# A recorded kernel's scheduling model with table loads and landing times, and one more query tile of stick-breaking attention turned by VectorE squares and a transfer

## The chip, the core and the metric

The kernel runs on one core of a Trainium2 chip. A core has a matrix engine (TensorE, PE in the profile), VectorE (DVE), ScalarE (ACT), GpSimd (POOL) and SyncE (SP), which here only issues transfers. Each engine works through its own queue of instructions in order; an instruction that waits holds up all behind it. The metric is device time in microseconds, the median over several runs; lower is better.

## What is computed

One layer of a hybrid encoder: 1024 prompt rows and 32 sample rows of width 1024. Cut to what matters here:

```python
def stick_breaking(q, k, v, q_pos, k_pos):
    z = jnp.einsum('bqhd,bkhd->bhqk', q, k).astype(jnp.float32) * ATTN_SCALE
    causal = (k_pos[None, :] < q_pos[:, None])[None, None]
    log_beta = jax.nn.log_sigmoid(z)
    log_1m = jnp.where(causal, jax.nn.log_sigmoid(-z), 0.0)
    after = lax.cumsum(log_1m, axis=3, reverse=True) - log_1m
    w = jnp.where(causal, jnp.exp(log_beta + after), 0.0).astype(v.dtype)
    return jnp.einsum('bhqk,bkhd->bqhd', w, v)

def reference(...):
        qa, ka, va, ga, qb, kb, vb, gb = in_proj(hp, g_pre[i], w_in[i])
        oa = mixer_a_prompt(qa, ka, va, rel_bias[i])
        ob = mixer_b_prompt(qb, kb, vb)
        hp = finish(hp, oa, ga, ob, gb, w_out[i], g_post[i], p_prompt[i], w_ple[i], w_ple_gate[i])
        ...
```

`in_proj` is an RMS norm and one projection to 4096 columns. Eight heads of width 64 (A) use banded softmax attention with a position bias, eight (B) the stick-breaking attention above. `finish` gates both results, projects them, normalizes, and adds a gated embedding. The sample rows go through the same, with caches of keys and values.

## The kernel before

**Stages.** After a start that normalizes and turns the input, the kernel goes through four pairs of heads of A and four of B in turn (A0, B0, A1, B1, ...; `B21` is the second head of pair 2 of B). Beside a pair's attention run the projection columns of the next pair (`mm_kA`, `mm_qB`, ... 24 matmuls of 352 columns for each third of the rows), and beside the last pair the gates (`mm_gA`, `mm_gB`). A last stage, closed off from the first, holds both square projections (`o0P` to `g3P`), in seven products of half-size blocks. All matrix work runs on numbers split into a high and a low part, so most things exist twice (`kd`/`kl`, `wTh`/`wTl`).

**A head of B.** Its 1024 queries are eight tiles of 128 rows; tile i sees i + 1 blocks of 128 keys. `scores(i)` (L828) makes two matmuls per piece into PSUM (`SB`), VectorE adds the mask of the diagonal block, ScalarE takes the sigmoid into `om`, VectorE runs a product scan backwards over it, and GpSimd subtracts neighbours into `be`: the weights, queries on the partitions. `weights_t(i)` (L878) turns them so that keys are on the partitions and splits them into `wTh` and `wTl`. `values(g)` (L928) multiplies the turned tiles 0 to 3 (g = 0) or 4 to 7 (g = 1) with V into `PVB`; it needs all four tiles of its group. A head of A is alike, with a bias, an exponential, and at most 5 blocks for a tile.

**Two ways to turn a tile.** The usual way: TensorE turns each 128x128 block against the identity into PSUM (`ptwB`, `ptwA`), up to four blocks to a bank; ScalarE casts the bank into `wTh`, VectorE subtracts that from the bank into `wTl`. The other way is for tiles named in `ROUND` (L31): VectorE turns 32x32 squares of the whole tile from `be` to `om`, SyncE writes `om` to a scratch tensor in HBM (`swapB<-om`), then reads it back by four transfers, one for each quarter of the partitions (`be<-swapB`); ScalarE casts `be` into `wTh`, and VectorE subtracts SBUF from SBUF into `wTl`. Before the change tiles 4 and 6 of each head, of A and of B, go this way. `om` and `be` are ring buffers (L517) of 3076 and 3328 columns for all heads; a tile's part is handed on when its last use is over. The PSUM pools have two banks for the projection (`mm`), three for scores, two for turned blocks, one for values (L473).

**What sets the order.** Nothing is issued as the code runs. `Recorder` (L264) notes each operation with its operands; `Recorder.add` (L308) finds what it depends on and calls `cost` (L338) for its duration and the delay until its result is usable. `Recorder.order` (L374) then simulates the five engines with these numbers: at each step the engine that is free first takes the ready operation with the smallest key (attention before projection columns on TensorE, then order of recording). The sequence that comes out is emitted as the program. So the constants in `cost` and `order` decide only in which order each engine's instructions stand. For a transfer, the model before takes `ISSUE` = 600 ns of SyncE's time, and lets data be there after a further 1500 ns, the time of the bytes, and a margin of 2000 ns. Loads of ScalarE's function tables are no operations of the recorder: they come into the program where `Exp` follows `Sigmoid` or the other way round, and the model before has no time for them. `shared` marks operations on the port that VectorE and GpSimd share.

Of the kernel before, what the change touches and what calls it, by code (L numbers as in the profile page):

```python
# [8 lines left out]
F32 = mybir.dt.float32  # L9
F32R = mybir.dt.float32r  # L10
AF = mybir.ActivationFunctionType
# [16 lines left out]

ROUND = {"A": ((4,),(6,)), "B": ((4,),(6,))}  # L31
LAG_T = 2
LAG_V = 2
SPACE_S = 0.1
# [138 lines left out]


class Op:
    __slots__ = ("eng", "what", "args", "kw", "key", "busy", "late", "ready", "left", "after", "at", "size", "shared")


LAND = {"PE": 165, "ACT": 0, "DVE": 0, "POOL": 0, "SP": 0, "CTL": 0}
SEM = 60  # L180
MARGIN = 400
ISSUE = 600
DMA_NS, DMA_RATE, DMA_MARGIN = 1500, 320.0, 2000
DVE_SET, POOL_SET = 137, 110


# [77 lines left out]
class Recorder:  # L264
# [35 lines left out]
    def node(self, eng, what, args, kw, after):  # L300
        o = Op()
        o.eng, o.what, o.args, o.kw, o.after = eng, what, args, kw, after
        o.key = (self.cls if eng == "PE" else self.low, len(self.ops))
        o.shared = False
        self.ops.append(o)
        return o

    def add(self, eng, what, args, kw):  # L308
        writes, reads = [], []
        method = what[1] if isinstance(what, tuple) else ""  # L310
        for i, a in enumerate(args):
            if isinstance(a, (View, Raw, Segments)):
                (writes if i == 0 or (method == "tensor_tensor_reduce" and i == 7) else reads).append(a)
        for k, a in kw.items():
            if isinstance(a, (View, Raw, Segments)):
                (writes if k in ("out", "accum_out") else reads).append(a)
        o = self.node(eng, what, args, kw, set())
        for mine, write in ((reads, False), (writes, True)):
            for v in mine:
                b = v.buf  # L320
                hit = False
                for other, box, wrote in b.uses:
                    if other is not o and (write or wrote) and all(p < y and x < q for (p, q), (x, y) in zip(v.box, box)):
                        o.after.add(other)
                        hit = True
                if b.pool is not None:
                    if not hit:
                        o.after.add(b.place)
                    b.pool.ops.append(o)
                b.uses.append((o, v.box, write))  # L330
        o.busy, o.late = self.cost(eng, method, args, kw, writes, reads)
        o.shared = eng == "POOL"
        if eng == "DVE":
            sbuf = [v for v in reads if isinstance(v, (View, Segments)) and not v.buf.psum and v.free() > 4]
            o.shared = len(sbuf) > 1 or (method == "tensor_copy" and len(sbuf) == 1 and not writes[0].buf.psum)

    @staticmethod
    def cost(eng, method, args, kw, writes, reads):  # L338

        out = writes[0] if writes else None  # L340
        n = out.free() if isinstance(out, View) else 1
        psum = any(isinstance(v, (View, Segments)) and v.buf.psum for v in reads)
        if eng == "PE":
            if method == "transpose":
                return (109 if args[1].shape[0] > 64 else 62), 165
            return max(109.0, 2.5 + 0.449 * args[2].free()) * (1 if args[2].buf.dtype == F32R else 4), 165
        if eng == "ACT":
            return (60 if psum else 95) + 0.83 * n + (190 if "accum_out" in kw else 0), 105
        if eng == "DVE":
            if method == "tensor_tensor_scan":  # L350
                return 120 + 2.1 * n, 85
            if method == "tensor_copy" and not psum:
                return 70 + 0.53 * n, 85
            if method == "scalar_tensor_tensor":
                return 125 + 1.04 * n, 85
            if method == "tensor_tensor_reduce":
                return 90 + 1.04 * n, 150
            return 70 + 1.04 * n, 85
        if eng == "POOL":
            if method == "tensor_tensor":  # L360
                if n == 1:
                    return 535, 40
                return 170 + (1.77 if out.buf.dtype == F32 else 2.15) * n, 40
            if method == "tensor_scalar":
                return 255 + 0.86 * n, 0
            return 100 + 0.82 * n, 0
        size, run = 4, 0
        for v in (out, args[1]):
            if isinstance(v, View) and v.buf.pool is not None:
                size, run = 4 * v.shape[0] * v.free(), 4 * v.shape[-1]  # L370
        return ISSUE, max(size / DMA_RATE, size / run * (8.5 + 0.0365 * run) / 16)


    def order(self):  # L374

        import heapq
        for place, old in self.turns:
            place.after.update(x[0] for x in old.uses)
        users = {id(o): [] for o in self.ops}
        for o in self.ops:  # L380
            o.left, o.ready = len(o.after), 0.0
            for a in o.after:
                users[id(a)].append(o)
        names = ("PE", "ACT", "DVE", "POOL", "SP", "CTL")
        free = dict.fromkeys(names, 0.0)
        soon = {e: [] for e in names}
        now = {e: [] for e in names}
        for o in self.ops:
            if not o.left:
                heapq.heappush(soon[o.eng], (0.0, o.key, id(o), o))  # L390
        out, port, line = [], 0.0, 0.0
        while len(out) < len(self.ops):
            best = None
            for e in names:
                if now[e]:
                    t = free[e]
                elif soon[e]:
                    t = max(free[e], soon[e][0][0])
                else:
                    continue  # L400
                if best is None or t < best[0]:
                    best = (t, e)
            t, e = best
            while soon[e] and soon[e][0][0] <= t:
                _, key, n, o = heapq.heappop(soon[e])
                heapq.heappush(now[e], (key, n, o))
            o = heapq.heappop(now[e])[2]
            if o.shared and e == "DVE" and port > t + DVE_SET:
                held = [x for x in now[e] if not x[2].shared]
                if held:  # L410
                    heapq.heappush(now[e], (o.key, id(o), o))
                    pick = min(held)
                    now[e].remove(pick)
                    heapq.heapify(now[e])
                    o = pick[2]
            o.at = t
            if e == "CTL":
                done = t
            elif e == "SP":
                free[e] = t + o.busy  # L420
                line = max(line, t + o.busy + DMA_NS) + o.late
                done = line + DMA_MARGIN
            else:
                if o.shared:
                    t = max(t, port - (DVE_SET if e == "DVE" else POOL_SET))
                    port = t + o.busy
                free[e] = t + o.busy
                done = t + o.busy + o.late
            out.append(o)
            for u in users[id(o)]:  # L430
                if u.eng == e and e != "SP":
                    r = t if e == "CTL" else free[e] if e == "PE" else done
                else:
                    r = done + (0 if u.eng == "CTL" else SEM + (MARGIN if u.eng == "PE" else 0))
                u.ready = max(u.ready, r)
                u.left -= 1
                if not u.left:
                    heapq.heappush(soon[u.eng], (u.ready, u.key, id(u), u))
        return out
# [18 lines left out]
def stream_step(  # L458
# [79 lines left out]
    def load_w(j):  # L538

        if j >= len(order) or j in raws:  # L540
            return
        kind, p = order[j]
        c0 = NAMES.index(kind) * 512 + p * P
        raws[j] = []
        for kh in range(2):
            raw = wpool.tile([P, 4, P], F32, tag="wr", name=f"wr_{kind}{p}_{kh}", bufs=4)
            dma(raw, w_in[0, kh * 512:(kh + 1) * 512, c0:c0 + P].rearrange("(k p) c -> p k c", p=P))
            raws[j].append(raw)
# [243 lines left out]
    def attention(ab, p, h):  # L792
# [16 lines left out]

        together = {i: g for g in ROUND[ab] for i in g}  # L810
        whole, done_with = {}, []
# [901 lines left out]
    for m, (nm, src, group) in enumerate(sets):  # L1713
        last_set = m == len(sets) - 1
        state = [{}, {}]
        for n, prod in enumerate(ORDER):
            for pair, t in enumerate(group):
# [43 lines left out]
                if nm == "o":  # L1761
# [4 lines left out]
                    if prod == "P6":  # L1766
                        add(up, st["p1"], bank, ALU.add)
# [101 lines left out]
```

## Time and profile before

| | us |
|---|---|
| median of 3 runs | 805.05 (804.86 to 805.52) |
| the profiled execution | 809.23 |
| its span, first to last instruction | 807.4 |
| ScalarE's table loads, 10 of 1283 ns | 12.8 |

The profile is of one execution. The span is 1.8 us shorter than that execution's own time, and the profiled execution is 4.2 us longer than the median of the others. The rows below are of these kinds: the page's busy time by engine and by slice (40 equal slices, each digit a busy share in tenths); busy time by stretch; waits (who waited for whom: us in total, times, longest); groups of instructions (engine, operation, `out<-in`, size, count | busy us, mean ns of one | idle time before them and what ended it); and the timeline (start us, duration us, engine, operation, count, and in brackets the idle time before it). `SPq` is SyncE's queue; a transfer's row there is its issue, and the rows of issues end with the median us from issue to landing. Matmuls are pipelined, so their durations overlap.

### The profile page before, as it was taken

The page shows a single profiled execution, that of the slowest core. Times are in us where ns is not written, and L with a number is a line of the kernel's source. Part 1 is how long each engine was busy: PE and PEld are TensorE (multiplying, and loading weights), DVE is VectorE, ACT ScalarE, POOL GpSimd, SP SyncE. Part 2 cuts the span into 40 slices and gives each one's busy share as a digit, 9 for nine tenths or more (in the row PEclk, how much of TensorE's full clock was granted, in tenths as well). Part 3 has the DMA queues.
Part 4 walks back from the last instruction along what each step waited for, and adds up shares of the span by engine and source line. Part 5 has one row for each costly group of instructions (what it writes and reads, how often), then busy time and mean ns, then how long its engine had stood idle before and what let it go on. Part 6 is the DMA issues. An engine that isn't in the chain of part 4 may idle for free.

```text
span 807.4 us, 14271 instructions
## 1 busy us (share of the span) xinstructions
PE 788.0 (98%) x4646; PEld 722.3 (89%) x4646; DVE 567.9 (70%) x1007; ACT 504.4 (62%) x1061; POOL 432.1 (54%) x503
## 2 busy tenths in 40 slices
PE   8999989999999999999999999999999999999997
PEld 7899989899989999899999989999997777878786
DVE  7626768786588788788886688765435787477655
ACT  5636774676586646795675696543327977877641
POOL 5623655764356668134551236777542549598513
PEclk9999999999999999999999999999999999999999
DMA  8419895667878749854535667765569948869633
GB/s 276 149 45 293 215 253 175 195 185 217 225 225 246 215 121 267 216 146 133 151 81 169 147 175 212 234 199 152 166 207 322 298 147 270 278 218 302 215 108 131
DMA packets 160973, 161.09 MB, mean 199 GB/s; under 512 B 39154, under 2 KB 120794, under 8 KB 160899
## 3 DMA queue, kind: packets, MB, share of 16 engines
q1 hardware_dynamic: 160898, 160.18, 67.1%
q8 instruction: 37, 0.61, 0.3%
q14 instruction: 38, 0.30, 0.1%
HBM read 99.23 MB, written 52.49 MB: 188 GB/s over the span
## 4 chain that ended last, share of the span: by engine, by line
PE 72%; DMA 6%; ACT 6%; POOL 5%; DVE 5%; issue 4%; SPq 2%; DVEq 0%; POOLq 0%; ACTq 0%
PE mm_gA L452 6%; PE mm_gB L452 6%; PE mm_kA L452 5%; PE mm_qA L452 5%; PE mm_qB L452 4%; PE SB L452 3%; PE mm_vA L452 3%; PE PVB L452 3%; PE mm_kB L452 3%; PE PVA L452 3%; PE mm_vB L452 3%; PE SA L452 2%; PE o1P L452 2%; PE g2P L452 2%; PE g3P L452 2%
## 5 line engine op out<-in xcount | busy, mean ns | idle before, releaser
L452 POOL TENSOR_TENSOR be<-om 128x128 f32<-128x128 f32 (+7 forms) x64 | 75.4, 1184 | 64.8 <-DVE om L452 29.0
L452 DVE TENSOR_TENSOR_SCAN om<-om,SB 128x384 f32<-128x384 f32 (+5 forms) x96 | 94.9, 1001 | 9.1 <-ACT om L452 7.4
L452 ACT ACTIVATE om<-SB 128x384 f32<-128x384 f32 (+5 forms) x96 | 44.4, 493 | 36.0 <-DVE SB L452 26.9
L452 ACT ACTIVATE be<-om,statA 128x640 f32<-128x640 f32 (+3 forms) x64 | 44.4, 694 | 18.2 <-DVE statA L452 11.0
L452 DVE TENSOR_TENSOR wTl<-be,wTh 128x640 fp32r<-128x640 f32 (+1 forms) x32 | 37.6, 1175 | 10.3 <-ACT wTh L452 8.8
L452 ACT CAST wTh<-ptwB 128x512 fp32r<-128x512 f32 (+3 forms) x64 | 29.5, 481 | 19.6 <-PE ptwB L452 15.4
L452 DVE TENSOR_TENSOR wTl<-ptwB,wTh 128x512 fp32r<-128x512 f32 (+3 forms) x64 | 33.7, 545 | 10.3 <-ACT wTh L452 7.8
L452 DVE TENSOR_TENSOR wTl<-ptwA,wTh 128x512 fp32r<-128x512 f32 (+2 forms) x64 | 29.8, 483 | 15.7 <-ACT wTh L452 12.5
L452 POOL TENSOR_TENSOR oB<-oB,oB 128x256 f32<-128x256 f32 x32 | 27.7, 882 | 18.6 <-DMA oB<-in_w_out_dram 10.5
L452 DVE STREAM_TRANSPOSE om<-be 128x640 f32<-128x640 f32 (+1 forms) x32 | 28.9, 904 | 9.8 <-POOL be L452 4.9
L452 PE MATMUL SB<-kdB,LB 128*128 128x384 f32 (+5 forms) x96 | 34.0, 357 | 1.6 <-DVE om L452 1.6
L452 DVE CUSTOM_DVE_ANT_0 om<-SA,biasA 128x320 f32<-128x320 f32 (+3 forms) x64 | 29.5, 482 | 7.6 <-PE SA L452 4.4
L452 ACT CAST wTh<-ptwA 128x512 fp32r<-128x512 f32 (+2 forms) x64 | 26.2, 426 | 13.3 <-PE ptwA L452 7.5
L452 PE MATMUL SB<-klB,LB 128*128 128x384 f32 (+5 forms) x96 | 32.9, 345 | 0.0
L452 PE MATMUL SA<-kdA,LA 128*128 128x320 f32 (+2 forms) x96 | 30.2, 325 | 0.7 <-DVE LA L452 0.4
L452 POOL TENSOR_TENSOR sggA<-sggA,oggA 128x352 f32<-128x352 f32 x24 | 23.8, 991 | 11.2 <-DVE sggA L452 10.8
L452 PE MATMUL SA<-klA,LA 128*128 128x320 f32 (+2 forms) x96 | 29.6, 320 | 0.0
L452 ACT CAST wTh<-be 128x640 fp32r<-128x640 f32 (+1 forms) x32 | 25.0, 782 | 6.4 <-DMA swapA<-om 3.3
L452 PE MATMUL ptwB<-ident,be 128*128 128x128 f32 x192 | 28.7, 273 | 0.0
L452 PE MATMUL ptwA<-ident,be 128*128 128x128 f32 x160 | 26.3, 276 | 2.0 <-ACT be L452 1.8
L452 DVE TENSOR_TENSOR SB<-SB,maskb 128x128 f32<-128x128 f32 x64 | 17.3, 287 | 13.5 <-PE SB L452 13.1
L452 POOL TENSOR_TENSOR klA<-stkA,kdA 64x1024 fp32r<-64x1024 f32 x8 | 20.7, 2587 | 8.2 <-ACT kdA L452 7.7
(707 smaller groups left out, 2650.5 us busy)
## 6 DMA issues: line engine op xcount, KB each, us to landing
swapA<-om SPq DMA_DIRECT2D x16, 320.0 KB, 2.8
be<-swapA SPq DMA_DIRECT2D x64, 80.0 KB, 3.9
oB<-in_w_out_dram SPq DMA_DIRECT2D x16, 256.0 KB, 4.9
sum_dro<-oB SPq DMA_DIRECT2D x16, 256.0 KB, 3.3
gB<-in_w_ple_gate_dram SPq DMA_DIRECT2D x16, 256.0 KB, 4.6
sum_drg<-gB SPq DMA_DIRECT2D x16, 256.0 KB, 3.8
x<-in_x_prompt_dram SPq DMA_DIRECT2D x16, 256.0 KB, 5.2
h_dr<-h SPq DMA_DIRECT2D x8, 512.0 KB, 3.3
```

Of the source, the lines that this page charges most:

```text
L452: getattr(getattr(tc.nc, o.what[0]), o.what[1])(*args, **kw)
```

## The change

Tile 5 of each head of B is added to the tiles turned by squares and a transfer, as a group of its own. In the model, a load of a function table takes 1310 ns of ScalarE when an exponential or a sigmoid follows the other; a transfer takes 500 ns to issue and lands 2050 ns after its bytes, with no further margin; most operations of ScalarE, VectorE and GpSimd take 30 ns more, and a GpSimd operation starts 90 ns later behind one of another engine.

```diff
--- before.py
+++ after.py
@@ -28,7 +28,7 @@
 
 
 
-ROUND = {"A": ((4,),(6,)), "B": ((4,),(6,))}
+ROUND = {"A": ((4,),(6,)), "B": ((4,),(5,),(6,))}
 LAG_T = 2
 LAG_V = 2
 SPACE_S = 0.1
@@ -173,14 +173,15 @@
 
 
 class Op:
-    __slots__ = ("eng", "what", "args", "kw", "key", "busy", "late", "ready", "left", "after", "at", "size", "shared")
+    __slots__ = ("eng", "what", "args", "kw", "key", "busy", "late", "ready", "left", "after", "at", "size", "shared", "table")
 
 
 LAND = {"PE": 165, "ACT": 0, "DVE": 0, "POOL": 0, "SP": 0, "CTL": 0}
 SEM = 60
 MARGIN = 400
-ISSUE = 600
-DMA_NS, DMA_RATE, DMA_MARGIN = 1500, 320.0, 2000
+ISSUE = 500
+DMA_RATE, LANDING = 320.0, 2050
+TABLE_NS = 1310
 DVE_SET, POOL_SET = 137, 110
 
 
@@ -301,7 +302,7 @@
         o = Op()
         o.eng, o.what, o.args, o.kw, o.after = eng, what, args, kw, after
         o.key = (self.cls if eng == "PE" else self.low, len(self.ops))
-        o.shared = False
+        o.shared, o.table = False, None
         self.ops.append(o)
         return o
 
@@ -330,6 +331,7 @@
                 b.uses.append((o, v.box, write))
         o.busy, o.late = self.cost(eng, method, args, kw, writes, reads)
         o.shared = eng == "POOL"
+        o.table = next((a for a in args if a in (AF.Exp, AF.Sigmoid)), None) if eng == "ACT" else None
         if eng == "DVE":
             sbuf = [v for v in reads if isinstance(v, (View, Segments)) and not v.buf.psum and v.free() > 4]
             o.shared = len(sbuf) > 1 or (method == "tensor_copy" and len(sbuf) == 1 and not writes[0].buf.psum)
@@ -345,22 +347,22 @@
                 return (109 if args[1].shape[0] > 64 else 62), 165
             return max(109.0, 2.5 + 0.449 * args[2].free()) * (1 if args[2].buf.dtype == F32R else 4), 165
         if eng == "ACT":
-            return (60 if psum else 95) + 0.83 * n + (190 if "accum_out" in kw else 0), 105
+            return (90 if psum else 125) + 0.83 * n + (190 if "accum_out" in kw else 0), 105
         if eng == "DVE":
             if method == "tensor_tensor_scan":
-                return 120 + 2.1 * n, 85
+                return 150 + 2.1 * n, 85
             if method == "tensor_copy" and not psum:
-                return 70 + 0.53 * n, 85
+                return 100 + 0.53 * n, 85
             if method == "scalar_tensor_tensor":
-                return 125 + 1.04 * n, 85
+                return 155 + 1.04 * n, 85
             if method == "tensor_tensor_reduce":
-                return 90 + 1.04 * n, 150
-            return 70 + 1.04 * n, 85
+                return 120 + 1.04 * n, 150
+            return 100 + 1.04 * n, 85
         if eng == "POOL":
             if method == "tensor_tensor":
                 if n == 1:
-                    return 535, 40
-                return 170 + (1.77 if out.buf.dtype == F32 else 2.15) * n, 40
+                    return 565, 40
+                return 200 + (1.77 if out.buf.dtype == F32 else 2.15) * n, 40
             if method == "tensor_scalar":
                 return 255 + 0.86 * n, 0
             return 100 + 0.82 * n, 0
@@ -388,7 +390,7 @@
         for o in self.ops:
             if not o.left:
                 heapq.heappush(soon[o.eng], (0.0, o.key, id(o), o))
-        out, port, line = [], 0.0, 0.0
+        out, port, line, table = [], 0.0, 0.0, None
         while len(out) < len(self.ops):
             best = None
             for e in names:
@@ -418,20 +420,23 @@
                 done = t
             elif e == "SP":
                 free[e] = t + o.busy
-                line = max(line, t + o.busy + DMA_NS) + o.late
-                done = line + DMA_MARGIN
+                line = max(line, free[e]) + o.late
+                done = line + LANDING
             else:
                 if o.shared:
                     t = max(t, port - (DVE_SET if e == "DVE" else POOL_SET))
                     port = t + o.busy
                 free[e] = t + o.busy
-                done = t + o.busy + o.late
+                if o.table and o.table != table:
+                    table = o.table
+                    free[e] += TABLE_NS
+                done = free[e] + o.late
             out.append(o)
             for u in users[id(o)]:
                 if u.eng == e and e != "SP":
                     r = t if e == "CTL" else free[e] if e == "PE" else done
                 else:
-                    r = done + (0 if u.eng == "CTL" else SEM + (MARGIN if u.eng == "PE" else 0))
+                    r = done + (0 if u.eng == "CTL" else SEM + (MARGIN if u.eng == "PE" else 90 if u.eng == "POOL" else 0))
                 u.ready = max(u.ready, r)
                 u.left -= 1
                 if not u.left:
```

## The prediction

> **What bounds the kernel now.** I read the page's busy shares and slices first, then the busy time by stretch, then who waits on TensorE.
>
> ```profile
> span 807.4 us, 14271 instructions
> PE 788.0 (98%) x4646; PEld 722.3 (89%) x4646; DVE 567.9 (70%) x1007; ACT 504.4 (62%) x1061; POOL 432.1 (54%) x503
> ...
> PE   8999989999999999999999999999999999999997
> ...
> DVE  7626768786588788788886688765435787477655
> ...
> DMA  8419895667878749854535667765569948869633
> ```
>
> TensorE is busy in every slice. No other engine comes near, though VectorE stands mostly at 7 and 8 tenths through the attention heads (the fifth to the twenty-sixth slice), and DMA reaches 9 tenths in the fourth, sixth and sixteenth slices. A busy matmul row includes pipeline overlap, so 98% is not a statement about peak, but it says that TensorE always has something in flight: what it no longer has to issue comes off the end, unless a new wait eats it.
>
> ```profile
> 56.00:135.00 79.00, 75.78 (x478) 72.93 (x477) 53.62 (x110) 52.24 (x112) 42.22 (x53) 0.98 0.81 226
> 310.00:395.00 85.00, 84.22 (x535) 80.00 (x534) 69.89 (x133) 58.87 (x129) 39.72 (x46) 1.00 0.68 185
> ```
>
> These columns are the stretch, its length, then busy time of PE, PEld, DVE, ACT, POOL, the granted clock, DMA share and GB/s. The first stretch holds heads A00 to B00 and leaves TensorE idle for 3.2 us; the second holds the two heads of pair B2, with 0.8 us.
>
> ```profile
> PE PVA L452 <- ACT wTh L452: 2.7, 1, 2.7
> PE ptwA L452 <- ACT be L452: 1.8, 2, 1.3
> PE SB L452 <- DVE om L452: 1.6, 3, 0.9
> PE ptkA L452 <- DVE wTl L452: 1.3, 1, 1.3
> PE PVB L452 <- ACT wTh L452: 0.3, 1, 0.3
> ```
>
> So TensorE's explicit waits in the attention are few and short. Only one of them, the first, is for weights turned through a transfer; B's second value product, which needs tiles 4 to 7 of the head, has waited 0.3 us in all.
>
> **Part 1: tile 5 of B leaves TensorE.** A head's tile 5 has 6 blocks of 128x128, so 8 heads x 6 = 48 transposes go (the built program holds 4600 matmuls against 4648).
>
> ```profile
> L452 PE MATMUL ptwB<-ident,be 128*128 128x128 f32 x192 | 28.7, 273 | 0.0
> 192.18 0.93 PE L452 MATMUL ptwA<-ident,be 128*128 128x128 f32 x7
> 192.86 1.54 PE L452 MATMUL mm_kB<-hnh,wh_kB 128*128 128x352 f32 x8
> 195.04 0.60 PE L452 MATMUL ptksA<-ident,be 128*128 128x128 f32 x4
> 195.40 0.57 PE L452 MATMUL mm_kB<-hnh,wl_kB 128*128 128x352 f32 x2
> ```
>
> The mean of 273 ns is a latency; transposes overlap. Seven of them delay the next matmul by 192.86 - 192.18 = 0.68 us, four by 0.36 us: 0.09 to 0.097 each. 48 x 0.09 = 4.3 us, 48 x 0.097 = 4.7; I take 4.4. The upper end is the busy union, 28.7 / 192 = 0.149 each, 7.2 us.
>
> The Trainium skill, "TensorE: Matmul & The Clock Gate", section "Part 4: PE-mode transpose", gives about 275 ns for a transpose inside a kernel, most of it access latency. The row's 273 ns agrees as a duration; taken as a cost it would make 13 us, which is case (3) below.
>
> **Part 2: what takes its place.**
>
> ```profile
> L452 DVE STREAM_TRANSPOSE om<-be 128x640 f32<-128x640 f32 x24 | 20.1, 836 | 7.7 <-ACT be L452 4.4 <-POOL be L452 3.2
> L452 DVE STREAM_TRANSPOSE om<-be 128x896 f32<-128x896 f32 x8 | 8.9, 1107 | 2.2 <-POOL be L452 1.7 <-POOL om L452 0.4
> L452 DVE TENSOR_TENSOR wTl<-be,wTh 128x640 fp32r<-128x640 f32 x24 | 26.3, 1097 | 6.6 <-ACT wTh L452 6.3
> L452 DVE TENSOR_TENSOR wTl<-be,wTh 128x896 fp32r<-128x896 f32 x8 | 11.3, 1410 | 3.7 <-ACT wTh L452 2.4 <-DMA out_dram<-vtA 0.9
> L452 DVE TENSOR_TENSOR wTl<-ptwB,wTh 128x512 fp32r<-128x512 f32 x32 | 21.4, 680 | 8.6 <-ACT wTh L452 6.2 <-PE PVB L452 2.4
> L452 DVE TENSOR_TENSOR wTl<-ptwB,wTh 128x256 fp32r<-128x256 f32 x16 | 6.6, 413 | 0.5 <-ACT wTh L452 0.4
> L452 ACT CAST wTh<-be 128x640 fp32r<-128x640 f32 x24 | 17.4, 726 | 4.9 <-DMA swapA<-om 3.3 <-DMA be<-swapA 1.3 <-PE PVB L452 0.2
> L452 ACT CAST wTh<-be 128x896 fp32r<-128x896 f32 x8 | 7.6, 948 | 1.5 <-DMA be<-swapB 1.5
> L452 ACT CAST wTh<-ptwB 128x512 fp32r<-128x512 f32 x32 | 18.4, 587 | 16.5 <-PE ptwB L452 12.7 <-PE PVB L452 3.5
> L452 ACT CAST wTh<-ptwB 128x256 fp32r<-128x256 f32 x16 | 6.0, 376 | 1.0 <-PE ptwB L452 0.9
> ```
>
> 768 columns lie halfway between 640 and 896. VectorE gains a turn, (836 + 1107) / 2 = 972 ns, and a subtraction from SBUF, (1097 + 1410) / 2 = 1254 ns, and loses 680 + 413 = 1093 ns: +1.13 us a head, +9.0 us over the eight. ScalarE gains (726 + 948) / 2 = 837 ns and loses 587 + 376 = 963: -1.0 us in all. VectorE had 85.00 - 69.89 = 15.1 us free in the two B2 heads' stretch, which covers the 2.3 us; I put 0. Without that cover it would be up to 9.0 us. GpSimd's work on the tile is unchanged.
>
> Weighed against this is a rule of the Trainium skill, "SBUF — State Buffer", section "Who interferes with whom": a VectorE instruction with two SBUF inputs and a GpSimd instruction that reads SBUF shut each other out for a whole instruction. It speaks against the new subtraction, which reads both inputs from SBUF where the old pair read one from PSUM.
>
> ```profile
> L452 DVE TENSOR_TENSOR wTl<-be,wTh x32: 799/826/2816, 91.5 to 577.6; 128x640 fp32r<-128x640 f32 x24, 128x896 fp32r<-128x896 f32 x8
> ```
>
> By that rule, the trace agrees: minimum 799 ns, longest 2816. Should each of the eight meet the longest, VectorE would pay some 8 x (2816 - 1254) = 12.5 us more, again beside TensorE.
>
> **Part 3: the round trip, and the new landing times.** A turned tile is written out by one issue and read back by four, on SyncE's queue: 40 more issues (824 DMAs in the program against 784).
>
> ```profile
> 419.00 1.11 DVE L452 STREAM_TRANSPOSE om<-be 128x896 f32<-128x896 f32 x1
> 420.14 0.35 SPq L452 DMA_DIRECT2D swapB<-om  x1
> 422.66 1.86 SPq L452 DMA_DIRECT2D be<-swapB  x4
> 430.31 0.94 ACT L452 CAST wTh<-be 128x896 fp32r<-128x896 f32 x1
> be<-swapB SPq DMA_DIRECT2D x32, 112.0 KB, 2.9
> ```
>
> SyncE spends 0.35 + 1.86 = 2.2 us a head on it, 18 us in all. Behind those issues in its queue stand the weight loads (`wr`), the writes of `o_dr` and the swap of V; the reads wait for the write's landing, the write for the squares of the tile, and whatever stands behind waits with them. In this round the last read was issued by 424.5; with 2.9 us to land it was there at about 427.2, while the cast started at 430.3: 3 us of slack, which the old model had put there (600 + 1500 + 2000 = 4100 ns and the data for each transfer). The new one allows 500 + 2050 = 2550, so 1.55 us less for each of two transfers and 0.4 for four issues, 3.5 us: the slack is spent, and casts will stand about where the data lands. Where the data comes late, ScalarE waits at the cast with all that is behind it (score sigmoids, PSUM copies), as here:
>
> ```profile
> 103.31 0.72 ACT L452 CAST wTh<-be 128x640 fp32r<-128x640 f32 x1 [3.30 <-DMA swapA<-om]
> 104.08 1.18 PE L452 MATMUL PVA<-wTh,v2A 128*128 128x512 f32 x3 [2.73 <-ACT wTh L452]
> ```
>
> There 3.30 us on ScalarE became 2.73 us on TensorE even under the old model. In the program's order the room shrinks too: from tile 6's last score to the second value product of its head TensorE has 124 matmuls in B21 (184 before), 138 in B11 (172), 135 in B00 (156); six of each difference are the transposes. Price: at least 0 (before, B's waits are 0.3), at most 3.5 us at each of the 8 B heads, 28. The value lies near the before end, since landing stays within the allowance in a round like the one shown: +1.5, half of one busy round.
>
> **Part 4: table loads and the other constants.**
>
> ```profile
> 474.55 1.28 ACT L452 ACT_TABLE_LOAD   x1
> ...
> 477.63 0.66 PE L452 MATMUL ptwA<-ident,be 128*128 128x128 f32 x4 [1.29 <-ACT be L452]
> ```
>
> The old model knew nothing of this load, and TensorE waited 1.29 us for an exponential behind it. The new one counts 1310 ns, but it doesn't choose by it: both programs hold ten loads. The triple switch that stood at the start of B30 is gone and one stands at the start of B10, where the model now knows of it. Between -1.8 (both `ptwA` waits gone) and +1.3 (the wait moves, one more stays): I take -0.8. The added 30 ns on ScalarE, VectorE and GpSimd and 90 ns before a GpSimd instruction redraw the order everywhere; no row prices that. Its room is the rest of the listed waits, 1.6 + 1.3 + 0.3 = 3.2 us to either side; I take 0.
>
> **Sum.** -4.4 + 0 + 1.5 - 0.8 + 0 = -3.7 us. The profiled execution took 809.2 us, 1.8 more than its span, and would take 805.5; the median of the runs is 805.05, which gives 801.4. With transposes at 7.2, 0 for landing and -1.8 the low end is 805.05 - 9.0 = 796. A measurement here tells apart about 0.2%, 1.6 us.
>
> **The rivals.**
> (1) *Slower: casts in line before their data.* For it: the spent slack and the shorter room in B11, B21, B00. Against it: outside the first stretch no `wTh` cast's wait reached TensorE for more than 0.3 us. If each B head's second value product waits 1.3 us, the longest ordinary wait listed, that is 10.4 - 4.4 = +6 us, 811; at 0.8 us a head, 807. It decides from about 0.75 us a head on.
> (2) *No change: the gain is given back in the reshuffled order.* 4.4 us is little against an order redrawn for 14271 instructions; two or three new waits like the 1.3 us ones do it: 803.5 to 806.6. Against it: the five waits listed above come to 7.7 us, so a redrawn order has as many old waits to lose as new ones to find.
> (3) *More than the cadence:* if a transpose costs its whole 273 ns, 13.1 us go and 792 remains. Against it: the next matmul starts 0.36 us after four of them.
> That the change does nothing is excluded for part 1 (the instructions are gone); for the table loads it is as said above: counted, not saved.
>
> **How the numbers follow.** Forecast (796 to 803.4) 0.54, slower 0.27, no change 0.17, more 0.02. So faster 0.56, within 0.2% 0.17, slower 0.27. The forecast's own range is 796 to 803.4; since cases of both signs hold much of the chance, the range given runs from 796 to 810, leaving out the last part of (1) and (3).
>
> **What would show it.** Right: 144 `ptwB` transposes; 8 turns and 8 subtractions of 768 columns at about 0.97 and 1.25 us; VectorE's busy time up by about 9 us; TensorE's busy time down by about 4 and its waits for `wTh` no longer than before; casts starting 0 to 1 us after the last landing. Wrong: `PVB <- ACT wTh` or `PVA <- ACT wTh` adding up to over 5 us, ScalarE waiting on DMA `be<-swapB` in most heads, or a TensorE idle total above the 19.4 us (807.4 - 788.0) of before by more than 4.

## The result and the profile after

The changed kernel took 810.52 us, the median of 14 runs (806.12 to 815.42), against 805.19 us of the kernel before beside it (14 runs): 1.006 of its time, with an interval from 1.004 to 1.008. It is slower by some 5 us, where 3.7 us less had been forecast; 810.5 lies just above the stated range (796 to 810) and at the top of the first rival (807 to 811).

The profiled execution of the changed kernel took 807.59 us, 2.9 less than its median, and that of the kernel before 809.23, 4.0 more than the 805.19 it had here. The two profiles therefore stand the wrong way round in length, and only their parts can be compared. From the page of the changed kernel, span and busy time:

```profile
span 805.8 us, 14283 instructions
PE 782.2 (97%) x4598; PEld 716.2 (89%) x4598; DVE 572.5 (71%) x1007; ACT 503.5 (62%) x1053; POOL 436.0 (54%) x503
```

TensorE is busy for 5.8 us less than before (788.0) and idle for 805.8 - 782.2 = 23.6 us, 4.2 more (19.4 before). So the work left, and in this execution most of its time came back as idle time. The stretch with the two B2 heads in the changed kernel, with the columns used before:

```profile
310.00:395.00 85.00, 80.88 (x509) 76.19 (x508) 68.02 (x131) 59.05 (x126) 36.12 (x42) 1.00 0.73 187
```

TensorE was idle for 0.8 us of it before and is for 4.1 now; of these only 0.6 us are a wait of a value product for turned weights. What TensorE waits for in the whole program (us in total, times, longest):

```profile
PE SA L457 <- DVE statA L457: 3.4, 4, 1.0
PE PVB L457 <- ACT wTh L457: 2.7, 4, 0.9
PE ptksA L457 <- DMA o_dr<-otB: 1.5, 1, 1.5
...
PE PVA L457 <- ACT wTh L457: 1.1, 3, 0.4
PE ptwA L457 <- DVE wTl L457: 1.0, 2, 0.8
```

B's second value product now waits 2.7 us in four places (0.3 in one before), and scores of A wait 3.4 us behind statistics (0.3 in one place before). On ScalarE the picture is plainer. Its waits on transfers, in the changed kernel:

```profile
ACT wTh L457 <- DMA be<-swapB: 15.2, 14, 2.5
...
ACT wTh L457 <- DMA be<-swapA: 6.2, 6, 1.8
```

From the same view of the kernel before, all rows in which such a cast waits for a transfer:

```profile
ACT wTh L452 <- DMA swapA<-om: 3.3, 1, 3.3
...
ACT wTh L452 <- DMA be<-swapB: 1.5, 1, 1.5
...
ACT wTh L452 <- DMA be<-swapA: 1.3, 2, 0.7
```

Casts that wait for a turned tile: 4 waits of 6.1 us before, 20 waits of 21.4 us now. The groups of instructions that the change touched:

```profile
L457 ACT CAST wTh<-be 128x640 fp32r<-128x640 f32 x24 | 17.4, 727 | 11.4 <-DMA be<-swapA 6.2 <-DMA be<-swapB 4.0 <-PE PVB L457 1.0
L457 PE MATMUL ptwB<-ident,be 128*128 128x128 f32 x144 | 21.7, 273 | 0.0
L457 ACT ACT_TABLE_LOAD x10 | 12.8, 1283 | 0.9 <-PEq L1862 0.7
L457 DVE TENSOR_TENSOR wTl<-be,wTh 128x640 fp32r<-128x640 f32 x24 | 24.4, 1016 | 8.7 <-ACT wTh L457 8.6
L457 DVE TENSOR_TENSOR wTl<-be,wTh 128x768 fp32r<-128x768 f32 x8 | 11.4, 1429 | 4.6 <-ACT wTh L457 4.6
L457 DVE TENSOR_TENSOR wTl<-be,wTh 128x896 fp32r<-128x896 f32 x8 | 9.0, 1131 | 6.1 <-ACT wTh L457 6.1
L457 DVE STREAM_TRANSPOSE om<-be 128x768 f32<-128x768 f32 x8 | 7.7, 967 | 2.0 <-POOL be L457 2.0
L457 ACT CAST wTh<-be 128x896 fp32r<-128x896 f32 x8 | 7.5, 938 | 5.5 <-DMA be<-swapB 5.5
L457 ACT CAST wTh<-be 128x768 fp32r<-128x768 f32 x8 | 6.7, 834 | 5.7 <-DMA be<-swapB 5.7
```

The last column is where to look: every shape of the casts from `be`, tiles 4 and 6 too, now has more idle time before it that a read-back ended. For 640 columns it is 6.2 + 4.0 us (1.3 before, and 3.3 for a write), for 896 columns 5.5 (1.5 before). One round, of head B11, in the timeline (start, duration, engine, operation, count, idle time before):

```profile
265.95 1.11 DVE L457 STREAM_TRANSPOSE om<-be 128x896 f32<-128x896 f32 x1
...
269.64 0.43 SPq L457 DMA_DIRECT2D swapB<-om  x1
270.11 2.18 SPq L457 DMA_DIRECT2D be<-swapB  x4
...
276.16 1.76 SPq L457 DMA_DIRECT2D be<-swapB  x4
...
281.10 0.94 ACT L457 CAST wTh<-be 128x896 fp32r<-128x896 f32 x1 [1.24 <-DMA be<-swapB]
...
282.09 1.20 PE L457 MATMUL PVB<-wTh,v2B 128*128 128x512 f32 x4 [0.89 <-ACT wTh L457]
```

Tile 6's squares are done at 267.06. Its write goes out at 269.64; then come tile 5's four reads, then other issues, and only at 276.16 tile 6's own reads, done being issued at 277.92: 10.9 us after the squares. The cast waits 1.24 us for them, and TensorE 0.89 us for the cast. Over the eight heads of B, the cast of tile 6 starts on average 12.7 us after its squares (14.7 in the kernel before), worked out from the two timelines: the order now has the casts 2.0 us nearer to the turn. The last read, meanwhile, is issued on average 9.6 us after the squares, hardly sooner than in the kernel before (10.0): the casts moved forward, and the data did not.

### The profile page after: what moved, and what is told of

Its sections match the earlier page's. It is cut to its first block, busy times and chain, and to the rows that moved or that the text cites. A ratio compares the mean times of both kernels' runs of the same rounds, so it can differ in the third digit from the quotient of the medians.

```text
span 805.8 us, 14283 instructions
## 1 busy us (share of the span) xinstructions
PE 782.2 (97%) x4598; PEld 716.2 (89%) x4598; DVE 572.5 (71%) x1007; ACT 503.5 (62%) x1053; POOL 436.0 (54%) x503
## 4 chain that ended last, share of the span: by engine, by line
PE 66%; DMA 16%; POOL 5%; SPq 3%; DVE 3%; ACT 3%; issue 3%; DVEq 0%; POOLq 0%; ACTq 0%
PE mm_vA L457 5%; PE mm_kA L457 5%; PE mm_gA L457 4%; PE mm_qA L457 4%; PE PVB L457 3%; SPq L457 3%; PE SB L457 3%; PE PVA L457 3%; PE mm_vB L457 3%; PE mm_qB L457 3%; PE mm_kB L457 3%; DMA be<-swapA 3%; PE g0P L457 2%; PE o1P L457 2%; PE o3P L457 2%
## 5 line engine op out<-in xcount | busy, mean ns | idle before, releaser
L457 POOL TENSOR_TENSOR be<-om 128x384 f32<-128x384 f32 (+6 forms) x64 | 77.9, 1223 | 68.5 <-DVE om L457 40.1
L457 DVE TENSOR_TENSOR wTl<-be,wTh 128x640 fp32r<-128x640 f32 (+2 forms) x40 | 44.9, 1122 | 19.4 <-ACT wTh L457 19.3
L457 ACT CAST wTh<-be 128x640 fp32r<-128x640 f32 (+2 forms) x40 | 31.6, 790 | 22.7 <-DMA be<-swapB 15.2
L457 DVE STREAM_TRANSPOSE om<-be 128x640 f32<-128x640 f32 (+2 forms) x40 | 36.5, 914 | 7.7 <-POOL be L457 4.6
L457 POOL TENSOR_TENSOR oB<-oB,oB 128x256 f32<-128x256 f32 x32 | 25.7, 822 | 23.8 <-issue 9.9
L457 PE MATMUL SB<-kdB,LB 128*128 128x384 f32 (+5 forms) x96 | 33.4, 352 | 0.9 <-DVE om L457 0.9
L457 ACT CAST wTh<-ptwB 128x512 fp32r<-128x512 f32 (+3 forms) x48 | 22.0, 482 | 12.8 <-PE ptwB L457 10.2
L457 POOL TENSOR_TENSOR gB<-gB,gB 128x256 f32<-128x256 f32 x32 | 25.4, 818 | 7.3 <-DMA gB<-in_w_ple_gate_dram 5.6
L457 DVE TENSOR_TENSOR wTl<-ptwB,wTh 128x512 fp32r<-128x512 f32 (+3 forms) x48 | 25.3, 541 | 2.9 <-PE PVB L457 1.7
L457 POOL MEMSET biasA<- 64x64 f32 x16 | 2.4, 147 | 41.7 <-DMA biasA<-r_dr 38.1
```

What stands on the lines that cost most here:

```text
L457: getattr(getattr(tc.nc, o.what[0]), o.what[1])(*args, **kw)
```

## The experiments

Eighteen kernels ran, in five batches, each beside runs of the kernel before on the same chip (804.3 to 805.8 us there). Since the batches used several chips, ratios to the kernel before are what can be compared; brackets hold the 95% interval. L-numbers are those of the profiles shown.

**Parts of the change alone.** First tile 5 out, model new; then the old model with tile 5.

```diff
 after.py
-ROUND = {"A": ((4,),(6,)), "B": ((4,),(5,),(6,))}
+ROUND = {"A": ((4,),(6,)), "B": ((4,),(6,))}
```

> The whole new model, tile 5 of B turned by TensorE as before. Theory (landing times without a margin put ScalarE's casts and the value products where the data only just is, and TensorE pays when it comes late): about as slow as the change or slower, 806 to 814 us against 805.2, with runs several us apart (before: 3.7 us from lowest to highest, the change: 9.3) and ScalarE's waits on DMA far above the 8.7 us of before, 25 us or more. Rival (the round trip of tile 5 is what costs): within 2 us of before, runs close together.

811.3 us, 1.0081 [1.0064, 1.0098].

```diff
 before.py
-ROUND = {"A": ((4,),(6,)), "B": ((4,),(6,))}
+ROUND = {"A": ((4,),(6,)), "B": ((4,),(5,),(6,))}
```

> The model of before, tile 5 of B turned by squares and a transfer. Theory: the 4.4 us of transposes come off and the margin of the old model hides the transfer: 799 to 804 us, ScalarE's waits on DMA near 9 us. Rival (tile 5's round trip costs): 806 us or more. Rival (every redrawn order costs some us): anywhere from 803 to 809.

812.23 us, 1.0091 [1.0068, 1.0114]. Either half alone loses as much as the whole or more, so the two losses can't be added, and neither half could be called the guilty one. Next the landing times: put back in the change, and then the new ones alone in the kernel before.

```diff
 after.py
-ISSUE = 500
-DMA_RATE, LANDING = 320.0, 2050
+ISSUE = 600
+DMA_NS, DMA_RATE, DMA_MARGIN = 1500, 320.0, 2000
...
-                line = max(line, free[e]) + o.late
-                done = line + LANDING
+                line = max(line, t + o.busy + DMA_NS) + o.late
+                done = line + DMA_MARGIN
```

> The change with the old landing times put back (600 to issue, 1500 ahead of the bytes, 2000 behind them); tile 5, table loads, the 30 and 90 ns stay. Theory: faster than the change by 5 us or more, 800 to 805, runs close together, ScalarE's waits on DMA under 15 us. Rival (tile 5, or the other constants, cost): 808 to 812 as the change.

806.47 us, 1.0017 [1.0003, 1.0032].

```diff
 before.py
-ISSUE = 600
-DMA_NS, DMA_RATE, DMA_MARGIN = 1500, 320.0, 2000
+ISSUE = 500
+DMA_RATE, LANDING = 320.0, 2050
...
-                line = max(line, t + o.busy + DMA_NS) + o.late
-                done = line + DMA_MARGIN
+                line = max(line, free[e]) + o.late
+                done = line + LANDING
```

> The kernel before with the new landing times alone (500 to issue, 2050 behind the bytes). Theory: slower than before by 3 to 10 us, 808 to 815, runs several us apart, ScalarE's waits on DMA 25 us or more. Rival (landing times are harmless, since transfers do land so): within 2 us of before.

823.11 us, 1.0241 [1.0218, 1.0265]. At this point the landing times looked like the cause: taken back, most of the loss goes; alone, they cost 18 us. But 18 us is more than three times the loss of the change that contains them, and the longest waits on TensorE in this kernel are for row sums of A, and not for a turned tile:

```profile
PE ptwA L452 <- ACT sumrowA L452: 7.0, 3, 3.7
```

ScalarE's waits on transfers, which the expectations also name, don't follow the times either. Over all rows they come to 21.0 us in the kernel before and 57.3 in the change (the 8.7 and 50 of the expectations are sums of the longest rows only). In these four kernels, in the order above, they are 41.4, 34.6, 33.4 and 45.5 us, at 811.3, 812.2, 806.5 and 823.1.

So the next batch asked what the remaining combinations do, whether more margin on top of the change helps, and how far a constant without meaning moves the time.

```diff
 after.py, with the old landing times as in the third experiment
-ROUND = {"A": ((4,),(6,)), "B": ((4,),(5,),(6,))}
+ROUND = {"A": ((4,),(6,)), "B": ((4,),(6,))}
```

> The kernel before with the table loads, the 30 ns and the 90 ns in its model, old landing times, tile 5 turned by TensorE. So far these constants stood beside gains of 12 us (landing alone 823.1, with them 811.3) and 6 us (tile 5 alone 812.2, with them 806.5). If they are a better model by themselves: 795 to 802 us. If the kernel before is simply a good draw of order and every other draw lies higher: 805 to 810.

804.64 us, 0.9997 [0.9982, 1.0011].

```diff
 before.py, with the new landing times as in the fourth experiment
-ROUND = {"A": ((4,),(6,)), "B": ((4,),(6,))}
+ROUND = {"A": ((4,),(6,)), "B": ((4,),(5,),(6,))}
```

> Tile 5 by transfer and the new landing times, without table loads and the 30 and 90 ns. If the landing times cost by themselves: well above tile 5 alone, 818 to 830 us. If costs of redrawn orders do not add up: 808 to 816.

827.89 us, 1.0274 [1.0252, 1.0297].

```diff
 after.py
-DMA_RATE, LANDING = 320.0, 2050
+DMA_RATE, LANDING = 320.0, 4050
```

> The change with 4050 ns in the place of 2050 for the landing, all else the same. Theory (the missing margin costs about 4 to 6 us): 802 to 807 us against 810.5 for the change, runs within 5 us, ScalarE's waits on DMA under 25 us (the change: about 50). Rival (order draws alone): 806 to 814, no nearer to before.

817.94 us, 1.0165 [1.0147, 1.0184]: with 2 us more allowed for every landing the time is worse, not better, and ScalarE still waits 40.6 us on transfers, where under 25 was expected. Its profile has one wait that has nothing to do with turned tiles, at the border to the last stage:

```profile
PE o0P L457 <- ACT oB L457: 7.2, 2, 6.5
```

```diff
 before.py
-SEM = 60
+SEM = 65
```

> The kernel before with 65 ns in the place of 60 for a semaphore in the model: nothing about table loads, landing or tile 5, only a redrawn order. If the order before is an ordinary draw: 802 to 808 us. If it is a good one and any redrawing costs: 807 to 815, which would be most of what the change lost.

807.91 us, 1.0042 [1.0026, 1.0058]. Five nanoseconds more for a semaphore in the model, and nothing else, cost over 3 us. That changes how all runs above are to be read, so the scatter was measured further, on the kernel before and on the change.

```diff
 before.py
-MARGIN = 400
+MARGIN = 410
```

> The kernel before with 410 in the place of 400 ns for the margin of TensorE in its model: a second redrawn order without meaning, for the spread of such draws. The first took 807.9. If draws lie about evenly around the kernel before: 800 to 806. If before is a good draw: 806 to 812.

818.75 us, 1.0161 [1.0134, 1.0188].

```diff
 before.py
-SEM = 60
+SEM = 55
```

> The kernel before with 55 in the place of 60 ns for a semaphore in its model: a third redrawn order of it without meaning. Redraws so far: 807.9 and 818.8 (before itself 804.8); three orders of the change: 808.5, 810.5, 812.8. If before is a favourable draw of its own model: 806 to 818 us again. If its model gives such times in most orders: 802 to 807.

811.66 us, 1.0079 [1.0062, 1.0095].

```diff
 before.py
-MARGIN = 400
+MARGIN = 390
```

> The kernel before with 390 in the place of 400 ns for TensorE's margin, a fourth redrawn order; expected as for the third: 806 to 818 us if before is a favourable draw, 802 to 807 if not.

818.16 us, 1.0151 [1.0132, 1.0171].

```diff
 after.py
-SEM = 60
+SEM = 65
```

> The change with 65 in the place of 60 ns for a semaphore in its model, a redrawn order without meaning (such redraws of before took 807.9 and 818.8). If the change's model is good and its order an ordinary draw: 804 to 816 us, about as much below as above 810.5. If the new model bears redrawing better because it fits the chip: 808 to 813.

808.49 us, 1.0044 [1.0026, 1.0062].

```diff
 after.py
-MARGIN = 400
+MARGIN = 410
```

> The change with 410 in the place of 400 ns for TensorE's margin, a second redrawn order of it; expected as for the first: 804 to 816 if draws scatter, 808 to 813 if they do not.

812.84 us, 1.0102 [1.0073, 1.0131]. Four redraws of the kernel before give 1.0042, 1.0161, 1.0079 and 1.0151, mean 1.011; three draws of the change give 1.006, 1.0044 and 1.0102, mean 1.007. In the traces of the four redraws of the kernel before, 41 to 48% of TensorE's 4646 places hold a matmul of another group than before. What such a redraw does looks like this, in the three longest rows of TensorE's waits with `MARGIN` 410:

```profile
PE PVA L452 <- DVE sumsA L452: 3.7, 1, 3.7
PE SB L452 <- DVE om L452: 2.5, 2, 1.4
PE mm_kB L452 <- ACT wh_kB L452: 1.7, 1, 1.7
```

None of these is a wait for a turned tile (waits of `PVA` for `wTh` come to 0.7 us in this kernel). The order of the kernel before is better than all four neighbours, and a constant of this model can't be judged by one order on either side: of the first seven experiments, all but the two with the new landing times in the old model (1.0241 and 1.0274) differ from the kernel before by no more, within the intervals, than edits that mean nothing.

Nor does the time that the casts of turned tiles are held rank the orders. It is 28.7 us in the change with `SEM` 65 (1.0044) and 34.2 with `MARGIN` 410 (1.0102), but 9.9 with tile 5 alone (1.0091) and 8.9 with the table loads and the 30 and 90 ns alone (0.9997). So what the held casts cost in one order has to be measured within that order.

**Without a redraw.** To learn what the held casts cost, the order has to be kept. In the next kernels the model sees the operations of the changed kernel and orders them as it did; only after that are casts and subtractions given another source, `hnh[0]`, the normalized input, which is there from the start. Their sizes and places stay; they wait for no transfer. In the traces of these kernels each of TensorE's 4598 places holds a matmul of the same group as in the change.

```diff
 weights_t, in after.py
+ early = f(hnh[0]).rearrange("p a b -> p (a b)")[:, 0:m * P]
+     .rearrange("p (g b q) -> p g b q", g=4, q=32)[:, :, first[x]:first[x] + cost(x), :]
  nc.scalar.copy(hi, src)
+ rec.ops[-1].args = (hi, early)
  nc.vector.tensor_tensor(lo, src, f(hi), ALU.subtract)
+ rec.ops[-1].args = (lo, early, f(hi), ALU.subtract)
```

> The order of the change, instruction for instruction; all transfers still run, but the casts and subtractions of turned tiles (40 of each) read the normalized input, which is long there, in the place of the transferred weights, so none waits for a landing. The attention weights of those tiles are thus wrong. Theory (casts in line before their data are what the landing times cost): at least 5 us faster than the change, 799 to 805 us, and runs close together. Rival (the cost sits in other transfers, weights and V, or in the order as such): 807 to 811.

804.17 us, 0.9995 [0.9977, 1.0014]. All transfers still run, and 1.0060 - 0.9995 = 0.0065, 5.2 us, are gone: the held casts cost that. A difference of two such ratios is good to about 2 us either way, by their two intervals. (The edit also lets the next tile be written into `be` without waiting for these casts. That share is not separated; in the rows of GpSimd its waits for `wTh` and `wTl` before it writes `be` go from 4.0 to 2.5 us.) The control is the same edit in the kernel before:

> The same edit in the kernel before (32 casts and subtractions unheld, same wrong weights in those tiles): the control. Theory: its casts waited only some 5 us on ScalarE, so TensorE gets little: 802 to 805 us. If it falls as far as the change's, the edit measures something else.

805.91 us, 1.0013 [1.0, 1.0027]: there the hold costs nothing that can be measured, so the edit itself gains nothing either. Now the same with tile 5's casts alone, and with those of tiles 4 and 6 alone.

```diff
 as above, but
+ if ab == "B" and i == 5:
+     rec.ops[-1].args = ...
```

> The order of the change; tile 5's transfers run as in the change, but its casts and subtractions (8 of each) read the normalized input and wait for no landing (tile 5's weights are wrong). Leaving the transfers out as well gave 803.7. If late data at tile 5's casts is the cost: 802 to 806 us. If the load of its 40 issues on SyncE's queue and of 6 MB on the DMA engines is the cost: 808 to 811.

808.97 us, 1.0052 [1.0033, 1.0072]: tile 5's own casts are worth 0.0008, 0.6 us, which can't be told from nothing.

```diff
 as above, but
+ if i != 5:
+     rec.ops[-1].args = ...
```

> The order of the change; the casts and subtractions of tiles 4 and 6 (32 of each, A and B) read the normalized input and wait for no landing (their weights are wrong), tile 5 waits as in the change. If tile 5 alone is what costs: 808 to 811 us. If any of the 40 rounds costs about alike: 804 to 807.

804.37 us, 0.9992 [0.9975, 1.001]: 0.0068, 5.5 us. What costs is not the new tile's casts, but those of tiles 4 and 6 (of A and of B), which were there before. The last kernel leaves tile 5's 40 transfers out and keeps tiles 4 and 6 held:

```diff
 as with tile 5's casts alone, and
  dma(dr, w0[:, 0:m * P])
+ if ab == "B" and i == 5:
+     rec.ops[-1].what = None
...
  dma(w1[32 * c:32 * c + 32].rearrange("k (g x) -> k g x", g=4), x)
+ if ab == "B" and i == 5:
+     rec.ops[-1].what = None
...
 emit
+ if o.what is None:
+     continue
```

> The order of the change, with tile 5's 40 transfers left out and its casts reading the normalized input (tile 5's weights are wrong); tiles 4 and 6 wait as in the change. If tile 5's own round trip eats its 4.4 us (its transfers in SyncE's queue, its late data): 803 to 807 us. If the landing times of all other transfers are the cost: 808 to 811.

803.74 us, 0.9987 [0.9967, 1.0007]; against the kernel in which those transfers run and tile 5 is unheld too, that is 1.0052 - 0.9987 = 0.0065, 5.2 us. So it takes both: the transfers of tile 5 and the hold of tiles 4 and 6. Taking away either gives the 5 us back. The same head B11, in the timeline of the kernel without tile 5's transfers:

```profile
268.17 1.10 DVE L459 STREAM_TRANSPOSE om<-be 128x896 f32<-128x896 f32 x1
...
271.36 0.45 SPq L459 DMA_DIRECT2D swapB<-om  x1
...
275.87 1.88 SPq L459 DMA_DIRECT2D be<-swapB  x4
...
281.78 0.93 ACT L459 CAST wTh<-be 128x896 fp32r<-128x896 f32 x1
```

From squares (269.27) to the last read's issue (277.75) it is 8.5 us here, 2.4 less than in the change, and the cast stands there without a wait. Over the eight heads of B it is 8.4 us on average, 1.2 less than in the change (9.6). Leaving the transfers out takes 40 issues out of SyncE's queue and 6 MB off the DMA engines at once, and no run has them apart. The rows speak for the queue where tile 6 is concerned: its reads land a median of 2.7 us after their issue with and without tile 5's transfers. Tile 4's reads of B take 3.3 us with them and 2.6 without. TensorE's waits for `wTh` fall in step. In the change they came to 2.7 + 1.1 = 3.8 us; with tile 5 alone unheld they are:

```profile
PE PVB L457 <- ACT wTh L457: 3.1, 4, 1.4
...
PE PVA L457 <- ACT wTh L457: 1.6, 4, 0.5
```

Without the transfers:

```profile
PE PVA L459 <- ACT wTh L459: 2.1, 5, 0.6
```

And with tiles 4 and 6 unheld:

```profile
PE PVB L457 <- ACT wTh L457: 0.5, 1, 0.5
```

These rows carry 2.6 us of the difference that the transfers make (4.7 to 2.1) and 3.3 us of that of tiles 4 and 6 (3.8 to 0.5); with all casts unheld no such row is left. The rest the trace doesn't put down to the casts, and ScalarE's own list is no good measure of it. With tile 5 alone unheld it reads:

```profile
ACT wTh L457 <- DMA be<-swapA: 6.7, 6, 2.2
ACT wTh L457 <- DMA be<-swapB: 5.9, 5, 1.5
```

Without the transfers:

```profile
ACT wTh L459 <- DMA be<-swapA: 7.9, 7, 2.4
ACT wTh L459 <- DMA be<-swapB: 4.6, 4, 2.0
```

12.6 us against 12.5, at times 5.2 us apart: by these two kernels, it matters less how long ScalarE waits in all than whether TensorE needs what it is held at.

## Why the prediction was wrong

Two terms of the sum failed. Part 3, put at +1.5 us, measured about 5: that is shown by runs. Part 4's term for the redrawn order, put at 0 without a row behind it, has to hold what is then still missing, about 4 us: that is worked out as a remainder.

**What bounds the kernel** was right: TensorE is busy for 97% of the span, and the waits added to it decided. Two readings were incomplete, without a part in the sum. DMA reaches 9 tenths in the 31st, 32nd and 37th slices too. And of the listed waits two, not one, were for weights turned through a transfer: the 0.3 us of `PVB` also stood behind a cast of tile 6.

**Part 1, -4.4 us, was right as far as a profile shows.** 144 `ptwB` transposes are left, each still 273 ns long as a row, and TensorE's busy time fell by 5.8 us, between the 4.4 taken and the 7.2 of the upper end (other matmuls' overlap changes it too). That the 273 ns are not the cost is borne out by this: 13.1 us did not go. No run takes the transposes away and leaves all else, so the 4.4 us themselves are not measured.

**Part 2, put at 0.** A turn of 768 columns takes 967 ns (972 predicted) and a cast 834 (837); the subtraction 1429 (1254 predicted). VectorE's busy time rose by 4.6 us and not 9, mostly because the older 32 subtractions took 4.2 us less (26.3 to 24.4 and 11.3 to 9.0). Whether the cover was enough is open: with all casts unheld TensorE still waits 3.1 us for VectorE's `statA` (0.3 before), which can be the order or the added work.

**Part 3, +1.5 us, was mis-sized: it measured 5.2 to 5.5, each within about 2 us.** The mechanism was the one described: the slack is spent and casts stand in line before their data. Of the prediction's three signs of failure two came: casts of B's tiles wait for their read-backs 14 times, and TensorE's idle total rose by 4.2 us; its waits for `wTh` came to 3.8 us, not over 5. Two things were wrong in the size. That whatever stands behind tile 5's issues waits with them was said, but not priced: these issues stand in SyncE's queue ahead of tile 6's reads, as in B11, and the hold that costs is that of tiles 4 and 6 (5.5 us against 0.6 for tile 5's). And the one round that it was priced from was the quickest of the eight: in the kernel before, squares to last read issued took 4.4 us there and 10.0 us on average.

**Part 4, -0.8 us for the tables and 0 for the redrawn order, failed at the second.** The two `ptwA` waits behind an exponential (1.8 us) are gone, with ten table loads in both programs, but `ptwA` now waits 1.0 us for `wTl`. The redraw was given a room of 3.2 us to either side, the sum of the waits then listed. Waits that are listed limit what a redraw can save; they say nothing of what it can add. Measured by edits without meaning, a redraw of the kernel before costs 3 to 13 us (0.0042 to 0.0161 of 805), and the change is a redraw too. With every held cast freed, the change still takes 804.2 us, 0.0005 under the kernel before, where the transposes alone should give 4.4 us. The remaining 4 us are put down to the new order, and no trace shows them. The one profiled execution with all casts unheld took 800.8 us, 3.4 under the median of its kernel:

```profile
span 799.0 us, 14227 instructions
PE 780.0 (98%) x4598; PEld 717.2 (90%) x4598; DVE 576.2 (72%) x1007; ACT 503.0 (63%) x1053; POOL 436.7 (55%) x503
```

TensorE is idle for 19.0 us there, and its listed waits add up to 13.8 us, as in the kernel before (19.4 and 13.8). What the trace does show is that they are other waits:

```profile
PE SA L457 <- DVE statA L457: 3.1, 5, 1.0
PE ptksA L457 <- DMA o_dr<-otB: 2.3, 1, 2.3
...
PE SA L457 <- DMA klA<-klA: 1.3, 2, 0.9
```

So the balance, against the kernel before and by the ratios: -4.4 us for the transposes, +5.2 for the held casts, and +4.0 for what is left make the +4.8 measured (0.006 of 805). The third term is the remainder between the first, which rests on the profile, and the run with all casts unheld. It was not measured by itself: a smaller gain from the transposes, VectorE's added work and the new order can each have a part in it, and the redraws only show that an order can cost this much.

**The rivals.** The first, casts in line before their data, gave 807 to 811 and hit the time, by the mechanism that it named for about half of the losses; that the number fits so well is luck. It asked for 1.3 us at each of the eight second value products; the row shows 2.7 us at four. The second, the gain given back in a reshuffled order, fits the remainder, though its time (803.5 to 806.6) is too low. Its argument against itself (a redrawn order has as many waits to lose as to find) was wrong: the order of before was a favourable one, and all four neighbours are slower. The third is excluded: TensorE's busy time fell by 5.8 us and not 13.1.

**What stays open.** Whether the new model is worse than the old one: the three draws of the change (mean 1.007) lie inside the scatter of the four redraws of before (mean 1.011). Old landing times with tile 5 (1.0017) and the tables without it (0.9997) look better, the new landing times in the old model (1.0241, 1.0274) worse, but each was drawn once. No version that computes the whole layer beat the kernel before beyond its interval.

## What to carry to other kernels

Where a program's order comes from a model, price "the model changes" by trying edits without meaning first (a constant moved by a few per cent): if they move the time by more than the change is to bring, the new order, and not the change, sets the result, and several draws are needed for each side. To find what a wait costs, keep the order and take only the wait's reason away. And price an added transfer at the transfers that run beside it or stand behind it in its issuer's queue too, and not at its own consumer alone.

## What the hardware showed that was not expected

A long idle time of TensorE can cost more than its length. The wait of 2.73 us at 104 us in the kernel before is followed by a stretch at a lower granted clock (last three columns: granted clock, DMA share, GB/s):

```profile
100.00:104.00 4.00, 1.35 (x9) 1.05 (x7) 0.24 (x1) 0.70 (x3) 2.65 (x3) 1.00 0.91 268
104.00:108.00 4.00, 3.92 (x14) 3.72 (x15) 3.11 (x4) 4.00 (x10) 1.74 (x5) 0.57 1.04 243
```

And the same in the kernel with `MARGIN` 410, behind the 3.7 us wait for `sumsA`:

```profile
240.00:244.00 4.00, 0.43 (x4) 0.19 (x2) 0.43 (x3) 3.90 (x9) 0.00 (x0) 1.00 0.96 305
244.00:248.00 4.00, 3.85 (x16) 3.58 (x17) 3.27 (x8) 3.84 (x7) 3.17 (x6) 0.63 0.48 157
```

Four microseconds at 0.57 and 0.63 give up 1.7 and 1.5 us of full-speed work; the waits in the changed kernel's two B2 heads, 0.9 us at most, left the clock of that stretch at 1.00. In the twenty profiles all eight waits of 2.5 us and more were followed by such a drop. The length alone doesn't settle it below that: a wait of 2.4 us at 194 us with tiles 4 and 6 unheld left the clock at 1.00, and one of 1.6 us at 66 us in the new model without tile 5 was followed by four microseconds at 0.62.

The clock goes with the spread of the changed kernel's runs: of its 14, the seven with a granted clock of 0.999 or more have a median of 807.6 us, the other seven (0.992 to 0.997) of 811.9. It is not so in every kernel: with `SEM` 55 the two groups have 811.7 and 811.3. The changed kernel's profile is one of the seven quicker ones, so it hides part of the loss.
